# A planner's estimate of VectorE's times, made again, in a two-layer decoder step on one core

## The chip, the core and the metric

The kernel runs on one core of a Trainium2 chip. The metric is the device time of one execution in microseconds (us). The kernel before takes 2676.59 us, the median of three runs (2676.18 to 2676.59). Five engines work side by side, each through its own queue in program order: TensorE (PE in the profile) multiplies matrices, VectorE (DVE) and ScalarE (ACT) compute element by element, GpSimd (POOL) does a few small copies, and SyncE (SP) issues nearly all transfers from and to HBM.

## The reference, cut to what matters

It is one inference step of a two-layer trunk for 256 prompt tokens and 8 x 8 sample tokens, 320 in all, which share all weights, in fp32:

```
layer 0: x += chunk_mlp(rmsnorm(x))      # z = gelu(h @ w_in); u, v = z; v = rmsnorm(v)
                                         # s = causal mix of v per 128-token chunk; (u * s) @ w_out
         x += conv_ffn(rmsnorm(x))       # a = h @ w_in (2 x 5632); causal conv over 3 tokens
                                         # (silu(gate) * up) @ w_out
layer 1: x += dsa(rmsnorm(x))            # q, k, v, iq, ik, iw = h @ w_in; q, k normalised; rope
                                         # score = sum_heads relu(iq . ik) * iw; top-k of 64 keys a query
                                         # softmax attention over the selected keys; @ w_o
         x += conv_ffn(rmsnorm(x))
```

The prompt's queries choose 64 of up to 256 keys, the sample's 66 of 264 (256 of them in a paged cache). The updated caches and states are outputs too. D_MODEL is 2048; there are 16 query heads and 4 key heads of 128, and 16 index heads of 64.

## The kernel before

Everything is held transposed, 128 features on the partitions and the 320 tokens along the free axis; a 2048-wide activation is 16 such tiles. The weights come from HBM in units of 1 MB (`raw`, 3 buffers, on SP's queue). Each unit is used in two halves. `split(n)` (line 1182 on) makes of a half a high part `wh` (ScalarE) and a low part `wl` (VectorE), both 128x1024; the activations are split likewise (`hh`, `hl` for normed inputs, `rh`, `rl` for the ring of inner activations), and each weight tile is multiplied in three passes: wh.hh, wh.hl, wl.hh. A half is eight such triples, 24 matmuls of 320 columns. `split(n + 2)` is issued at the start of half n.

The weight matmuls are a list of groups of (mostly) 512 output columns: first the gMLP (v, u, down-projections in three parts), then ConvFFN 0, then the attention layer (index queries, index key, k, v, four q groups, four output groups per key head), then ConvFFN 1. A group's output columns rotate through six PSUM banks `mm`; a new column needs the bank of the sixth column before it, so `S.ensure(("ev", nbank - 6))`. Two more banks, `sd`, serve the small matmuls.

All the rest is side work, written as generators: norm tiles, the norm's end (`norm_fin`: sum over features by a matmul with ones, then 3 Newton iterations for the reciprocal root), the gating, the convolution (`ff_tile`), the index scores and their top-k search (`index_prompt`, `index_sample`, `topk`), rope, attention, key and value loads. They enter the queues by `Side.pump()`, called after every second triple: it advances a clock by SLOT = 0.82 us and lets each task that is ready take one step. A task's first step after it is added as urgent (the reading of a PSUM column) always runs. Other steps wait while `full()`, that is while the planned load of DVE or ACT is over BACKLOG = 3.0 us ahead of the clock; steps without small matmuls also wait until their inputs' planned end is near the clock (AHEAD), those with small matmuls until it is SLACK = 0.9 us behind it, and at most two of these run in a pump. Where the main loop needs something that is not made yet, `ensure` pumps on until it is: its instructions then stand ahead of the next matmul, which really waits for them.

The loads come from prices. Every engine object is wrapped (`Engine`, line 149 for all its instructions in the profile): before it issues an instruction it calls `side.op(key, price(name, n))`, with n the elements of the output per partition. In `op` the operation ends at max(engine free, the task's last end + LATENCY) + its price, and the engine's load is set to that end. The price of `dve.max` (8 largest values) goes by its output of 8 columns.

Two places to know for the prediction. In the last down-projection of the gMLP (and in the attention's last output groups) each half of 24 matmuls completes two columns of x; each is added to x (`resid`) and then normed (`norm_tile`: ScalarE's hh and square, then VectorE's hl and the sum of squares). The first ConvFFN groups need `("h", st, kt)` for kt 0 to 15 in order, a half using four of them, two column pairs after each other; its columns can be read only after `norm_fin` has set `("rs", st)`. In the attention layer, `index_done` waits for both searches and for the key ropes (`"k"`); it adds the attention tasks, which first issue the loads of cached keys and values on SP's queue. `k_done` stores new_kT, then `fold(1)` loads the rope tables (c_ropeT) again and multiplies them by the q gain (`"gq"`), after which the q columns can be roped and give their buffers (`tB`, four) back.

Of the kernel before, what the change touches and what calls it, by code (L numbers as in the profile page):

```python
# [33 lines left out]
AHEAD = 0.3  # L34
SLACK = 0.9
STEPS = 2
LATENCY = 0.1
PE = -1


# [5 lines left out]
class Side:  # L46
# [21 lines left out]
    def op(self, key, t):  # L68
# [8 lines left out]
        if key == "dma":  # L77
# [3 lines left out]
            return  # L81
        end = max(free, c.t + LATENCY if c else 0.0) + t
        self.load[key] = end
# [48 lines left out]
class Engine:  # L132
# [5 lines left out]
    def __getattr__(self, name):  # L138
        f = getattr(self.engine, name)
        if name == "value_load":  # L140
            return f

        def call(*a, **k):
            out = k["out"] if "out" in k else a[0]
            n = 1
            for d in out.shape[1:]:
                n *= d
            self.side.op(self.key, self.price(name, n))
            return f(*a, **k)  # L149

        return call
# [4 lines left out]


def dve_price(name, n):
    return (n * (0.6 if name in ("tensor_copy", "tensor_scalar", "memset") else 1.04) + 90) / 1e3


def act_price(name, n):
# [12 lines left out]
def trunk(ctx: ExitStack, tc: tile.TileContext, i, o):  # L175
# [3 lines left out]
    pool = Engine(nc.gpsimd, S, "pool", pool_price)  # L179
    sp = Engine(nc.sync, S, "dma", dma_price)  # L180
    dve = Engine(nc.vector, S, "dve", dve_price)
    act = Engine(nc.scalar, S, "act", act_price)

# [1140 lines left out]
```

## Time and profile before

| | before |
|---|---|
| median of 3 runs | 2676.59 us |
| profiled execution, its own time | 2677.56 us |
| its span | 2675.8 us |
| TensorE busy | 2652.6 us (99%) |
| VectorE busy | 1603.3 us (60%) |
| ScalarE busy | 1130.5 us (42%) |
| granted TensorE clock, mean | 0.997 |
| DMA | 405.70 MB, mean 152 GB/s |

The span is the time from the profile's first to its last instruction; the execution's own time is a little longer. Matmuls overlap in the array, so a busy TensorE is one that has work, not one at its peak. The side work and all weight splits share one source line (149), so instructions are told apart by the tiles that they write and read: `wl`, `wh` are the splits, `mm` the weight matmuls, `sd` the small ones, `xT` the residual, `hl` the norm's low half, and `arena` everything else of the side work.

### The profile page before, as it was taken

How to read it: one execution, taken by the hardware profiler on the slowest of the kernel's cores; microseconds unless marked ns; L12 is line 12 of the kernel's file. 1: busy time of each engine (PE TensorE's matmuls, PEld its weight loads, DVE VectorE, ACT ScalarE, POOL GpSimd, SP SyncE). 2: the span in 40 equal slices, each digit the busy share in tenths (PEclk: the TensorE clock that was granted, in tenths of full speed). 3: DMA queues.
4: the chain of work that ended last, by engine and by line, in shares of the span. 5: the costliest groups of instructions: out<-in, count | busy, mean ns of one | idle time of the engine just before them, and what ended most of it. 6: DMA issues, size and time to landing. Idle time of an engine off the chain costs nothing.

```text
span 2675.8 us, 44338 instructions
## 1 busy us (share of the span) xinstructions
PE 2652.6 (99%) x18174; PEld 2621.7 (98%) x18174; DVE 1603.3 (60%) x2803; ACT 1130.5 (42%) x1572; POOL 135.1 (5%) x370
## 2 busy tenths in 40 slices
PE   8999999999999999999999999999999999999999
PEld 8999999999999999999998989999999999999999
DVE  6465577646645564566668676776555645654663
ACT  5433344434433443344453554544344434433442
POOL 0000001001000010010000000000000000100100
PEclk9999999999999999999999999999999999999999
DMA  6444454444444444444543644444444444444444
GB/s 230 142 144 141 143 170 142 153 147 151 149 153 146 153 147 154 146 151 161 173 147 99 198 144 145 134 156 158 142 156 144 158 142 157 142 158 142 157 157 132
DMA packets 220284, 405.70 MB, mean 152 GB/s; under 512 B 9330, under 2 KB 33394, under 8 KB 219826
## 3 DMA queue, kind: packets, MB, share of 16 engines
q1 hardware_dynamic: 219794, 402.58, 46.2%
q8 instruction: 142, 2.33, 0.4%
q14 instruction: 60, 0.49, 0.1%
q10 hardware_dynamic: 288, 0.30, 0.0%
HBM read 396.69 MB, written 6.16 MB: 151 GB/s over the span
## 4 chain that ended last, share of the span: by engine, by line
PE 94%; DVE 3%; DMA 1%; ACT 1%; SPq 1%; issue 1%; ACTq 0%; DVEq 0%
PE mm L149 91%; PE sd L149 3%; DVE arena L149 2%; DVE wl L149 1%; SPq L149 1%; DMA arena<-a_v_norm 0%; ACT wh L149 0%; ACT arena L149 0%; DMA raw<-a_w_in 0%; DMA out_new_v_prompt<-arena 0%; DMA raw<-b_w_in 0%; DVE xT L149 0%; ACT rh L149 0%; DVE rl L149 0%; ACTq L149 0%
## 5 line engine op out<-in xcount | busy, mean ns | idle before, releaser
L149 DVE TENSOR_TENSOR wl<-raw,wh 128x1024 fp32r<-128x1024 f32 (+1 forms) x724 | 883.5, 1221 | 862.4 <-ACT wh L149 861.5
L149 ACT ACTIVATE wh<-raw 128x1024 fp32r<-128x1024 f32 (+1 forms) x724 | 764.6, 1057 | 1257.6 <-PE mm L149 1054.6
L149 PE MATMUL mm<-hh,wh 128*128 128x320 f32 x3856 | 1200.7, 311 | 10.5 <-DVE arena L149 9.9
L149 PE MATMUL mm<-hh,wl 128*128 128x320 f32 x3856 | 1192.2, 309 | 2.7 <-DVE wl L149 2.7
L149 PE MATMUL mm<-hl,wh 128*128 128x320 f32 x3856 | 1191.7, 309 | 0.0
L149 PEld LDWEIGHTS mm<-hh,wh 128*128 128x128 f32 x3856 | 726.0, 188 | 18.1 <-issue 15.6
L149 PEld LDWEIGHTS mm<-hh,wl 128*128 128x128 f32 x3856 | 725.8, 188 | 4.2 <-DVE wl L149 4.2
L149 PEld LDWEIGHTS mm<-hl,wh 128*128 128x128 f32 x3856 | 726.1, 188 | 0.7
L149 PE MATMUL mm<-rh,wh 128*128 128x320 f32 x1920 | 597.5, 311 | 0.0
L149 PE MATMUL mm<-rh,wl 128*128 128x320 f32 x1920 | 593.4, 309 | 0.0
L149 PE MATMUL mm<-rl,wh 128*128 128x320 f32 x1920 | 593.3, 309 | 0.0
L149 PEld LDWEIGHTS mm<-rh,wh 128*128 128x128 f32 x1920 | 360.7, 188 | 1.2 <-issue 1.0
L149 PEld LDWEIGHTS mm<-rl,wh 128*128 128x128 f32 x1920 | 360.7, 188 | 0.2
L149 PEld LDWEIGHTS mm<-rh,wl 128*128 128x128 f32 x1920 | 360.4, 188 | 0.0
L149 ACT ACTIVATE arena<-arena 128x336 f32<-128x336 f32 (+6 forms) x464 | 243.8, 540 | 148.3 <-DVE arena L149 144.7
L149 POOL COPY arena<-arena 128x16 f32<-128x16 f32 (+1 forms) x352 | 127.7, 401 | 1962.6 <-DVE arena L149 1544.6
L149 DVE SCALAR_TENSOR_TENSOR arena<-arena 128x336 f32<-128x336 f32 (+5 forms) x436 | 220.4, 510 | 9.2
L149 DVE TENSOR_TENSOR xT<-mm,xT 128x320 f32<-128x320 f32 x240 | 116.1, 487 | 81.4 <-PE mm L149 81.2
L149 DVE TENSOR_TENSOR arena<-arena 128x320 f32<-128x320 f32 (+6 forms) x413 | 146.4, 385 | 25.0 <-ACT arena L149 13.6
L149 DVE TENSOR_TENSOR arena<-mm,arena 128x64 f32<-128x64 f32 (+2 forms) x417 | 127.5, 343 | 47.6 <-PE mm L149 47.4
L149 PE MATMUL sd<-arena 128*128 128x128 f32 (+7 forms) x718 | 101.6, 318 | 6.6 <-DVE arena L149 3.3
L149 PEld LDWEIGHTS sd<-arena 128*128 128x128 f32 (+2 forms) x718 | 73.3, 157 | 22.0 <-issue 7.3
(36 smaller groups left out, 390.6 us busy)
## 6 DMA issues: line engine op xcount, KB each, us to landing
raw<-f_w_in SPq DMA_DIRECT2D x176, 1024.0 KB, 5.1
raw<-f_w_out SPq DMA_DIRECT2D x88, 1024.0 KB, 5.1
raw<-b_w_in SPq DMA_DIRECT2D x33, 1024.0 KB, 5.3
raw<-a_w_in SPq DMA_DIRECT2D x31, 1024.0 KB, 5.5
raw<-a_w_out SPq DMA_DIRECT2D x16, 1024.0 KB, 5.1
raw<-b_w_o SPq DMA_DIRECT2D x16, 1024.0 KB, 5.2
arena<-cache_kT SPq DMA_DIRECT2D x64, 64.0 KB, 2.0
arena<-cache_v SPq DMA_DIRECT2D x64, 64.0 KB, 2.0
```

Of the source, the lines that this page charges most:

```text
L149: return f(*a, **k)
```

## The change

Three prices of the planner are changed: LATENCY from 0.1 to 0.2; the fixed part of every DVE operation from 90 to 150 ns, and for `match_replace` (the search's second half) to 290 ns; and `max` is counted by the width of its input instead of its output of 8. No instruction is added or taken away; the order in which the side work stands in the queues is planned with the new figures.

```
-LATENCY = 0.1
+LATENCY = 0.2
...
-            out = k["out"] if "out" in k else a[0]
+            out = k["in_"] if name == "max" else k["out"] if "out" in k else a[0]
...
 def dve_price(name, n):
-    return (n * (0.6 if name in ("tensor_copy", "tensor_scalar", "memset") else 1.04) + 90) / 1e3
+    if name == "match_replace":
+        return (n * 1.04 + 290) / 1e3
+    return (n * (0.6 if name in ("tensor_copy", "tensor_scalar", "memset") else 1.04) + 150) / 1e3
```

## Rows read from the trace of the kernel before

**Rows 1.** The page's first part: engine, busy us (share of the span), instructions.

```profile
PE 2652.6 (99%) x18174; PEld 2621.7 (98%) x18174; DVE 1603.3 (60%) x2803; ACT 1130.5 (42%) x1572; POOL 135.1 (5%) x370
```

**Rows 2.** Stretches: length, busy PE, PEld, DVE, ACT, POOL, PE clock, DMA share, GB/s.

```profile
409.00:1315.00 906.00, 905.61 (x6175) 905.64 (x6176) 524.66 (x836) 374.51 (x467) 64.09 (x174) 1.00 0.46 151
...
1428.00:1476.00 48.00, 46.23 (x298) 41.60 (x296) 45.38 (x123) 16.75 (x28) 0.00 (x0) 1.00 0.34 110
1476.00:1506.00 30.00, 29.70 (x201) 29.34 (x200) 12.63 (x18) 12.29 (x20) 0.00 (x0) 1.00 0.76 245
...
1547.00:1562.00 15.00, 12.21 (x86) 9.35 (x85) 10.67 (x43) 9.82 (x28) 0.25 (x2) 0.92 0.48 145
1562.00:1592.00 30.00, 28.14 (x223) 25.04 (x222) 22.45 (x77) 16.76 (x38) 0.15 (x1) 0.98 0.42 126
```

**Rows 3.** Waits of PE: for whom, us in total, times, longest.

```profile
PE mm L149 <- DVE arena L149: 9.9, 3, 8.2
...
PE mm L149 <- DVE wl L149: 2.7, 5, 0.7
```

**Rows 4.** PE's time line, head and ConvFFN starts: start, us, instruction [idle before].

```profile
48.48 0.61 PE L149 MATMUL mm<-hh,wh 128*128 128x320 f32 x1 [8.20 <-DVE arena L149]
...
49.15 0.47 PE L149 MATMUL mm<-hh,wl 128*128 128x320 f32 x1
49.42 0.47 PE L149 MATMUL mm<-hh,wh 128*128 128x320 f32 x1
...
398.13 0.70 PE L149 MATMUL sd<-arena 128*128 128x320 f32 x2
...
409.39 0.39 PE L149 MATMUL mm<-hh,wh 128*128 128x320 f32 x1 [0.87 <-DVE arena L149]
...
1774.58 0.39 PE L149 MATMUL mm<-hh,wh 128*128 128x320 f32 x1 [0.87 <-DVE arena L149]
```

**Rows 5.** VectorE's time line at the first ConvFFN's start.

```profile
392.50 0.54 DVE L149 SCALAR_TENSOR_TENSOR hl<-xT,arena,hh 128x320 fp32r<-128x320 f32 x1
...
398.39 1.23 DVE L149 TENSOR_TENSOR wl<-raw,wh 128x1024 fp32r<-128x1024 f32 x1 [2.29 <-ACT wh L149]
...
400.78 0.49 DVE L149 TENSOR_TENSOR arena<-arena 128x320 f32<-128x320 f32 x1
401.30 1.02 DVE L149 SCALAR_TENSOR_TENSOR arena<-arena 128x320 f32<-128x320 f32 x2
...
408.69 1.94 DVE L149 TENSOR_TENSOR arena<-mm,arena 128x256 f32<-128x256 f32 x8
```

**Rows 6.** Groups by line and form, DVE: count, busy us, mean ns, idle before.

```profile
L149 DVE TENSOR_TENSOR wl<-raw,wh 128x1024 fp32r<-128x1024 f32 x720 | 880.8, 1224 | 861.2 <-ACT wh L149 860.3
```

**Rows 7.** VectorE's time line in the attention stage.

```profile
1434.02 0.42 DVE L149 MAX8 arena<-arena 128x8 f32<-128x256 f32 x1
...
1435.00 0.43 DVE L149 MAX8 arena<-arena 128x8 f32<-128x256 f32 x1
...
1497.37 0.89 DVE L149 TENSOR_SCALAR arena<-arena 128x320 f32<-128x320 f32 x2 [0.32 <-DMA arena<-c_ropeT]
...
1512.48 0.48 DVE L149 TENSOR_TENSOR arena<-mm,arena 128x320 f32<-128x320 f32 x1
```

**Rows 8.** The chain that ended last: start, us, engine and tile, instructions.

```profile
1774.58 897.84 PE mm L149 x6120
```

**Rows 9.** SP's queue in the attention stage: start, us, transfers issued.

```profile
1475.49 0.50 SPq L149 DMA_DIRECT2D out_new_kT<-arena  x1
...
1478.25 6.77 SPq L149 DMA_DIRECT2D arena<-cache_kT  x8
...
1494.99 0.91 SPq L149 DMA_DIRECT2D arena<-c_ropeT  x2
```

**Rows 10.** PE's time line in the attention stage.

```profile
1515.59 0.64 PE L149 MATMUL sd<-arena 128*32 128x256 f32 x8
...
1558.65 4.23 PE L149 MATMUL sd<-arena 128*128 128x128 f32 x14 [2.10 <-DVE arena L149]
```

## The prediction

> **What bounds the kernel now.** First the page's engine lines: TensorE is busy 2652.6 of a span of 2675.8 us [rows 1]. The matmuls of the weight groups fix the length; all else must fit beside them, and the 23 us in which TensorE stands still are what a better order can win. Second, the table by stretches of time, for where they lie: in the first ConvFFN (409 to 1315 us) TensorE misses 0.4 of 906 us; in 1428 to 1476, where VectorE (DVE) runs the top-k search, DVE is busy 45.4 of 48 us and TensorE misses 1.8; it misses 0.3 in 1476 to 1506, 2.8 in 1547 to 1562 and 1.9 in the 30 us behind that [rows 2]. Third, TensorE's waits: 9.9 us for DVE's arena work in three waits, of which one is 8.2 long, and 2.7 us for the low halves wl of the split weights [rows 3]. Fourth, TensorE's own time line: the 8.2 us are the first norm's tail at 48.48; the other two, 0.87 each, stand at 409.39 and 1774.58, the starts of the two ConvFFNs [rows 4].
>
> So three places can move: the two ConvFFN starts, which are alike, and the attention stage (1390 to 1592). Instructions, bytes and matmuls stay the same; the prices only set in which order the planner writes side work into the queues.
>
> **What the change does to the prices.** A DVE operation of 320 columns is priced 320 x 1.04 + 90 = 423 ns before and 483 after; one that hangs on the operation before it costs 0.523 and then 0.683 with LATENCY, which goes into DVE's load. In the norm's iterations the first such operation starts at 400.78 and its successor at 401.30: 0.52 us apart [rows 5]. The bare price becomes right, the chained one 30% too dear. A split of 1024 columns goes from 1.155 to 1.215; measured 1.224 [rows 6], right. A search round over 256 columns goes from 0.098 + 0.356 + 2 x 0.1 = 0.654 to 0.416 + 0.556 + 2 x 0.2 = 1.372; the trace has 1434.02 to 1435.00, 0.98 us [rows 7]: 33% too cheap before, 40% too dear after. All 25 rounds (8 of 256 columns, 9 of 264, 8 of 128): 15.3 before, 32.3 after. The 256 and 264 rounds at 0.98 and the 128 ones at some 0.7 (my estimate, scaled from these rows) make 22.
>
> An over-priced DVE does this: when its planned load is more than 3.0 us ahead of the clock, the planner holds every task that is not urgent. The side work then comes later against the matmuls, until a matmul needs it; there the planner pumps on without TensorE's progress, and TensorE really waits.
>
> [...]
>
> **Term 1, the ConvFFN starts.** In the eight halves of the last down-projection each half plans a split and two columns, each a residual add and a norm step (low half of h, sum of squares): 1.155 + 2 x (0.423 + 0.946) = 3.89 us before, 1.215 + 2 x (0.483 + 1.166) = 4.51 after, against 4 pumps x 0.82 = 3.28 us of clock. So the planned load overruns in both and the norm tiles are held. The extra: 16 x 0.28 for the columns, 0.54 for the four memsets of the ConvFFN's preparation, some 13 x 0.06 for splits, 5.8 us together. It drains at 3.28 - 1.215 = 2.07 a half, so the last tile comes 2.8 halves later: a half is 24 matmuls, 24 x 0.147 = 3.52 us [rows 8], so 10 us. Now the last low half is made at 392.50 [rows 5]. It is needed in the first group's seventh half, three halves ahead of the stall at 408.4 (409.39 less its gap), so at some 397.8. Slack 5, delay 10: the planner must make it there, behind that half's split, which ends at 399.6 [rows 5]. TensorE waits 1.2 to 2.4 us.
>
> Then the norm's reduction: 5.6 us from the last tile to its matmul (398.13, [rows 4]), and evictions at 408.69, 16 us from that tile [rows 5]. From about 400.3 this would end at 416, while the second group's second half, which needs a freed PSUM bank, comes at 408.4 + 2 = 410.4. What is left is then written in one go behind a split: two or three iterations of 1.56, a split 1.22, evictions 0.5 to 1, so 5.9 to 7.4 us of stall where there are 0.87 idle, 1.2 with the refill, now [rows 4]. Per start +1.2 to 2.4 and +4.7 to 6.2, so 5.9 to 8.6; I take 7, twice: **+14**. Bounds: the stalls of 1.2 vanish (-2.4), or the upper ends and a slow clock at both (2 x 8.6 + 2 x 2.9 = +23).
>
> On that clock: after the 8.2 us gap matmuls start 0.27 apart (49.15, 49.42) [rows 4] instead of 0.147 (897.84 / 6120, [rows 8]). 24 slow matmuls cost 24 x 0.12 = 2.9 us, and I keep that for the upper bound. [...]
>
> **Term 2, attention.** Search +17.0 and the 32 score accumulations +32 x 0.16 = 5.1: at least 22 us of planned DVE work more between 1390 and 1476, where the planner already holds. Of 0.82 us a pump the splits take 1.215 / 4 = 0.30; 22 / 0.52 = 42 pumps, or 37 us of TensorE's progress, by which the end of search and key work (new_kT is stored at 1475.49, [rows 9]) slides. Two matmul points wait for it. First, the third q group's second half needs a bank of the second q group, whose columns wait for the first group's rope buffers, and those for the query tables (c_ropeT). In the trace its first eviction is at 1512.48 [rows 7], and that half runs six matmuls behind the row at 1515.59 [rows 10], at about 1517: slack 4.5 us, far under 37. The wait holds what is left of the key ropes, 2 to 3 us; the tables, issue to use 2.4 us and more (1494.99 to 1497.37 [rows 7, 9]); one rope and an eviction, 2.5: some 7 to 8. The 24 cache loads that SP issues from 1478.25 to 1494.9, ahead of the tables [rows 9], add up to 17 if they fall into the wait again. Second, the first output group waits for attention 0 already now: its last 14 small matmuls take 1558.65 to 1562.9 and hold a wait of 2.10 for DVE [rows 10]. Starting later it is short by 5 to 8 more. The values' transposes, behind the search, may stall q0's banks for 0 to 5. Against it stand shorter waits for wl, 2 to 3 us of the 2.7 [rows 3] and of the 1.8 in 1428 to 1476 [rows 2]. Sum 7.5 + 6.5 + 2.5 - 2.5 = 14, and a quarter of the 17 for the loads: **+18**. Bounds: all of TensorE's idle time there gone (1.8 + 0.3 + 2.8 + 1.9 = -6.8), or everything at its upper end with the loads (+40).
>
> **Sum.** 14 + 18 = 32 on the profiled execution of 2677.6 is 2709.6; the median lies 1 us under it: 2709. The head (48.48) and the ConvFFNs' steady parts, where DVE has slack, cost nothing.
>
> **Rivals.** (1) Both places pay, my forecast: 2709, its own range 2695 to 2722; 0.45. (2) Only the ConvFFN starts pay, since search held back fills DVE's idle time in 1476 to 1506 (busy 12.6 of 30, [rows 2]) and the tables go ahead of the cache loads: 2677 + 14 = 2691; 0.18. (3) The cache loads fall in the wait whole: 2709 + 13 to 20, about 2726; 0.12. (4) The order hardly changes because urgent tasks and forced ones carry it, so the change doesn't do what it says: 2677, within 5; 0.10. For it speaks that most of the run is steady; against it that the plan is over its bound at all three places. (5) The other side: truer split and eviction prices bring wl in time and the idle 6.8 us in attention go with the 2.4 of the starts, 2677 - 9 = 2668; 0.15. It decides on the slack of 5 us at the ConvFFN starts: if the delay is under 1.4 halves instead of 2.8, no start pays, and term 2 must be nil too.
>
> 0.2% (5.4 us) is about what can be told from no change. Slower: 0.45 + 0.18 + 0.12 = 0.75; same 0.10; faster 0.15. The range 2671 to 2736 leaves out the better part of (5) and the worst of (3), about 0.2.
>
> **What would show it.** Right: TensorE waits for DVE at both ConvFFN starts, a short one for hl in the first group and one of 5 us or more in the second; a new wait in the third q group; DVE less dense in 1434 to 1476 and its search running past 1490; the wait for attention 0 longer. Wrong: the last hl still at least 3 us ahead of its use, search ending by 1480, or new idle time somewhere else, say in the gMLP's gating (before 376 us), for which I plan none.

## The result and the profile after

The changed kernel takes 2734.39 us, the median of four runs (2732.93 to 2736.72), against 2676.39 for the kernel before (2676.0 to 2676.59): the ratio is 1.0217, 95% interval 1.0205 to 1.0229, so 58 us slower. The forecast was 2709, with a range of 2671 to 2736.

The page's first part, of the profiled execution after the change (it answers to [rows 1]):

```profile
span 2732.7 us, 44318 instructions
...
PE 2671.2 (98%) x18174; PEld 2634.5 (96%) x18174; DVE 1618.0 (59%) x2803; ACT 1126.2 (41%) x1572; POOL 77.8 (3%) x370
```

The span grew by 56.9 us; the matmuls are the same 18174. The stretches that answer to [rows 2], and three new ones (length, busy PE, PEld, DVE, ACT, POOL, clock, DMA share, GB/s):

```profile
1428.00:1476.00 48.00, 48.00 (x336) 43.68 (x335) 36.13 (x71) 18.48 (x27) 0.00 (x0) 1.00 0.34 110
1476.00:1506.00 30.00, 30.00 (x207) 27.85 (x207) 21.35 (x57) 13.60 (x28) 0.00 (x0) 1.00 0.44 134
1506.00:1533.00 27.00, 20.13 (x123) 17.45 (x121) 21.56 (x55) 8.51 (x12) 0.00 (x0) 0.90 0.65 208
1561.00:1598.00 37.00, 24.59 (x131) 15.90 (x130) 21.13 (x87) 20.83 (x58) 0.42 (x2) 0.63 0.26 78
...
1572.00:1583.00 11.00, 9.82 (x50) 6.33 (x50) 6.15 (x36) 5.71 (x17) 0.16 (x1) 0.50 0.07 19
```

DVE is no longer dense in 1428 to 1476 (36.1 us instead of 45.4), and TensorE misses nothing there, nor in 1476 to 1506. The loss comes behind that: 6.9 us missed in 1506 to 1533, and 12.4 in 1561 to 1598, at a mean granted clock of 0.63. TensorE stands still for 8.99 us up to 1572.28, and in 1572 to 1583 its clock is 0.50.

TensorE's waits (answers to [rows 3]; us in total, times, longest):

```profile
PE mm L149 <- DVE arena L149: 23.4, 4, 8.2
PE sd L149 <- DVE arena L149: 19.9, 6, 9.0
PE mm L149 <- DVE hl L149: 3.8, 4, 1.7
PE mm L149 <- DVE rl L149: 1.8, 2, 0.9
PE mm L149 <- DVE wl L149: 1.8, 4, 0.7
```

Waits for DVE's arena work more than tripled (43.3 us of mm and sd together; before, 9.9 of mm and 3.3 of sd), and waits for hl are new; the gain in the waits for wl is 0.9 us. TensorE's time line at both ConvFFN starts, at the third q group and at the first output group (answers to [rows 4, 10]; in brackets the idle time before the instruction):

```profile
392.65 0.41 PE L149 MATMUL mm<-hl,wh 128*128 128x320 f32 x1 [1.75 <-DVE hl L149]
...
406.91 0.70 PE L149 MATMUL sd<-arena 128*128 128x320 f32 x2
417.99 0.60 PE L149 MATMUL mm<-hh,wh 128*128 128x320 f32 x1 [5.97 <-DVE arena L149]
418.39 0.47 PE L149 MATMUL mm<-hl,wh 128*128 128x320 f32 x1
418.66 0.47 PE L149 MATMUL mm<-hh,wl 128*128 128x320 f32 x1
...
1248.38 0.42 PE L149 MATMUL mm<-rh,wh 128*128 128x320 f32 x1 [0.53 <-ACT rh L149]
1249.68 0.41 PE L149 MATMUL mm<-rl,wh 128*128 128x320 f32 x1 [0.88 <-DVE rl L149]
...
1527.79 2.47 PE L149 MATMUL sd<-arena 64*128 64x320 f32 x4 [4.12 <-DVE arena L149]
1533.46 0.61 PE L149 MATMUL mm<-hh,wh 128*128 128x320 f32 x1 [3.20 <-DVE arena L149]
...
1572.28 2.66 PE L149 MATMUL sd<-arena 128*128 128x128 f32 x12 [8.99 <-DVE arena L149]
...
1597.08 0.41 PE L149 MATMUL mm<-rh,wh 128*128 128x320 f32 x1 [0.53 <-ACT rh L149]
...
1710.71 0.61 PE L149 MATMUL sd<-arena 128*128 128x128 f32 x3 [4.23 <-DVE arena L149]
...
1802.71 0.41 PE L149 MATMUL mm<-hl,wh 128*128 128x320 f32 x1 [1.70 <-DVE hl L149]
...
1828.02 0.60 PE L149 MATMUL mm<-hh,wh 128*128 128x320 f32 x1 [5.97 <-DVE arena L149]
```

The two ConvFFN starts are alike to 0.05 us: a wait for hl and one of 5.97 for the norm's end, where there were 0.87. After the latter, matmuls start 0.27 apart (418.39, 418.66), as after the long wait in the head. The pair at 1248 to 1250 is new as well: the last down-projection of ConvFFN 0 begins before its last inner tiles are made; ConvFFN 1 has the same.

VectorE's and SP's time lines that go with it (answers to [rows 5, 7, 9]):

```profile
392.05 0.55 DVE L149 SCALAR_TENSOR_TENSOR hl<-xT,arena,hh 128x320 fp32r<-128x320 f32 x1
...
400.04 0.55 DVE L149 SCALAR_TENSOR_TENSOR hl<-xT,arena,hh 128x320 fp32r<-128x320 f32 x1
...
414.14 0.48 DVE L149 TENSOR_TENSOR arena<-arena 128x320 f32<-128x320 f32 x1
...
415.71 0.49 DVE L149 TENSOR_TENSOR arena<-arena 128x320 f32<-128x320 f32 x1
...
417.29 1.94 DVE L149 TENSOR_TENSOR arena<-mm,arena 128x256 f32<-128x256 f32 x8
...
1525.79 0.42 DVE L149 MAX8 arena<-arena 64x8 f32<-64x264 f32 x1
...
1556.73 0.17 DVE L149 TENSOR_TENSOR arena<-arena 128x10 f32<-128x10 f32 x1
1556.93 0.38 DVE L149 SCALAR_TENSOR_TENSOR arena<-arena 128x10 f32<-128x10 f32 x2
```

```profile
1511.07 0.51 SPq L149 DMA_DIRECT2D out_new_kT<-arena  x1
1518.87 0.39 SPq L149 DMA_DIRECT2D raw<-b_w_in  x1
1519.30 0.98 SPq L149 DMA_DIRECT2D arena<-c_ropeT  x2
...
1526.53 4.84 SPq L149 DMA_DIRECT2D arena<-cache_kT  x8
```

The sixteenth low half comes at 400.04 instead of 392.50, the first evictions at 417.29 instead of 408.69, the sample's search ends at 1526 and new_kT is stored 36 us later.

To add this up, take the start of the n-th weight matmul (counted from 0) in each run's trace and subtract that of the kernel before. Four stages: up to the 2304th (the gMLP), the 8640th (ConvFFN 0), the 10992nd (attention) and the last one (ConvFFN 1). Differences in us:

| run | gMLP | ConvFFN 0 | attention | ConvFFN 1 | all | median, ratio (95%) |
|---|---|---|---|---|---|---|
| changed kernel | -0.5 | +12.6 | +32.3 | +12.4 | +56.8 | 2734.39, 1.0217 (1.0205 to 1.0229) |
| LATENCY alone (e1) | +0.4 | +8.1 | +4.9 | +6.4 | +19.9 | 2697.61, 1.0078 (1.0061 to 1.0094) |
| fixed part alone (e2) | -0.2 | +7.6 | +3.2 | +7.4 | +17.9 | 2694.85, 1.0070 (1.0053 to 1.0087) |
| search alone (e3) | -1.1 | 0.0 | +28.5 | 0.0 | +27.4 | 2704.61, 1.0104 (1.0087 to 1.0121) |
| LATENCY and fixed part (e4) | -0.5 | +13.5 | +25.5 | +12.2 | +50.7 | 2730.81, 1.0204 (1.0187 to 1.0221) |
| search, tables first (e5) | 0.0 | 0.0 | +18.4 | 0.0 | +18.3 | 2696.08, 1.0077 (1.0060 to 1.0094) |
| changed, bound 6.0 (e6) | -0.7 | +6.9 | +22.5 | +7.5 | +36.2 | 2714.31, 1.0143 (1.0126 to 1.0160) |
| measured prices (e7) | +0.2 | +7.4 | +20.9 | +7.0 | +35.5 | 2708.70, 1.0116 (1.0099 to 1.0133) |
| measured prices, clock 0.88 (e8) | -1.2 | -1.1 | +10.7 | -1.1 | +7.3 | 2688.49, 1.0047 (1.0030 to 1.0063) |
| the same, bound 6.0 (e9) | +2.7 | -1.1 | +9.6 | -1.1 | +10.0 | 2687.57, 1.0041 (1.0028 to 1.0055) |
| before, tables first (e10) | -0.4 | 0.0 | -6.7 | 0.0 | -7.1 | 2670.25, 0.9976 (0.9966 to 0.9986) |
| before, clock 0.92 (e11) | -2.3 | -1.1 | -0.2 | -1.1 | -4.8 | 2673.23, 0.9990 (0.9981 to 0.9999) |
| before, clock 0.88, bound 4.0, tables first (e12) | -0.8 | -1.1 | +2.3 | -1.1 | -0.7 | 2676.98, 1.0000 (0.9991 to 1.0009) |

Stages are those of one profiled execution, which need not be the median one: that of e4 lies 2.5 us under its median, that of e7 4.4 over it and that of e8 3.6 under it. The last column is of all runs, against those of the kernel before on the same chip (2675.86, 2676.42 and 2676.65 in three sets).

### The profile page after: what moved, and what is told of

Same layout as the page of the kernel before. It is cut to its first block, busy times and chain, and to the rows that moved or that the text cites. A ratio compares the mean times of both kernels' runs of the same rounds, so it can differ in the third digit from the quotient of the medians.

```text
span 2732.7 us, 44318 instructions
## 1 busy us (share of the span) xinstructions
PE 2671.2 (98%) x18174; PEld 2634.5 (96%) x18174; DVE 1618.0 (59%) x2803; ACT 1126.2 (41%) x1572; POOL 77.8 (3%) x370
## 3 DMA queue, kind: packets, MB, share of 16 engines
q1 hardware_dynamic: 219794, 402.58, 45.4%
## 5 line engine op out<-in xcount | busy, mean ns | idle before, releaser
L149 ACT ACTIVATE arena<-arena 128x336 f32<-128x336 f32 (+7 forms) x464 | 239.4, 539 | 127.8 <-DVE arena L149 125.5
L149 PE MATMUL sd<-arena 128*128 128x128 f32 (+8 forms) x718 | 108.8, 341 | 24.3 <-DVE arena L149 19.9
L149 POOL COPY arena<-arena 128x18 f32<-128x18 f32 (+1 forms) x352 | 69.9, 237 | 2019.2 <-DVE arena L149 1589.8
```

## The experiments

**The three prices one by one.** The theory: the planner's load for chained VectorE work is too high, so that it holds side work back until a matmul must wait. The rival: the search's price carries attention's loss alone, and the small fixed terms do little.

```
e1:  -LATENCY = 0.1                       e2:  -... else 1.04) + 90) / 1e3
     +LATENCY = 0.2                            +... else 1.04) + 150) / 1e3
```

> The kernel before with LATENCY 0.2 alone. Theory (planned load of chained VectorE work holds the side work back): a norm step costs 0.1 more in the plan, 16 x 0.1 + 0.3 for the memsets = 1.9 us at 2.13 a half, 0.9 halves later, so each ConvFFN start loses 1 to 3 us, attention 8 to 15 in the wait for attention 0; about 2692. Rival (the search's new price carries the loss in attention, the small fixed terms little): under 2682.

> The kernel before with the fixed part 150 alone. Theory: 16 x 0.12 + 0.24 + 13 x 0.06 = 2.9 us planned more, 1.4 halves, so each ConvFFN start loses 1 to 3 us; attention 8 to 15; about 2690. Rival (search's price): under 2682.

Both lie some 5 us above the theory's total (+21.7 and +19.0 by the medians), and its parts are off by more. The ConvFFN starts lose more than the 1 to 3 us expected. In the run with LATENCY alone:

```profile
393.58 0.41 PE L149 MATMUL mm<-hl,wh 128*128 128x320 f32 x1 [1.30 <-DVE hl L149]
414.92 0.39 PE L149 MATMUL mm<-hh,wh 128*128 128x320 f32 x1 [4.39 <-DVE arena L149]
```

With the fixed part alone there is no wait for hl, and the same 4.39 for the norm's end. Attention loses only 3 to 5, less than the 8 to 15 expected. By its number (under 2682) the rival falls with both, but through the ConvFFN starts; what it says of attention is not touched before e4.

```
e3:  +            out = k["in_"] if name == "max" else k["out"] if "out" in k else a[0]
     ...
     +    if name == "match_replace":
     +        return (n * 1.04 + 290) / 1e3
```

> The kernel before with the two search prices alone (max by its input, match_replace + 290). Theory: both ConvFFN starts stay as before (0.87 us of idle each), the search slides by some 33 pumps, a new wait in the third q group and a longer one for attention 0, together 10 to 20; about 2690. Rival (the search carries nearly all of attention's loss): 30 us or more in attention, 2706 or more.

The starts stay to the tenth, as expected; attention loses 28.5, between the theory's 10 to 20 and the rival's 30. One wait makes half of it, and SP's time line shows what it hangs on:

```profile
1527.94 0.60 PE L149 MATMUL mm<-hh,wh 128*128 128x320 f32 x1 [14.41 <-ACT arena L149]
```

```profile
1502.19 0.50 SPq L149 DMA_DIRECT2D out_new_kT<-arena  x1
1502.89 6.89 SPq L149 DMA_DIRECT2D arena<-cache_kT  x8
1509.96 4.64 SPq L149 DMA_DIRECT2D arena<-cache_v  x8
1514.78 3.93 SPq L149 DMA_DIRECT2D arena<-cache_kT  x8
...
1519.26 0.97 SPq L149 DMA_DIRECT2D arena<-c_ropeT  x2
```

The tables wait for 24 cache loads, my third rival. In the changed kernel they go ahead of the loads (1519.30 against 1526.53), so there this isn't the cause.

```
e4: the changed kernel with
-            out = k["in_"] if name == "max" else k["out"] if "out" in k else a[0]
+            out = k["out"] if "out" in k else a[0]
-    if name == "match_replace":
-        return (n * 1.04 + 290) / 1e3
```

> The changed kernel with the search's old prices (LATENCY 0.2 and the fixed part 150 stay). Theory: the ConvFFN starts lose all that they lose with the whole change, 12 us each, and attention most of its loss, since attention 0 itself is made of chained small operations: 2720 to 2733. Rival (search carries attention's loss): only the two starts, about 2701.

As the theory said: 2730.81, of the 58 us all but some 3; with that the rival falls for attention too. The search's price, which costs 28.5 by itself, adds little on top of the other two: 3 us by the medians, 6.8 in attention by the traces (32.3 - 25.5, with e4's trace 2.5 under its median). The losses in attention don't add. As I read it, without a run that shows it, each slides the end of the key work and of the search against matmul points that are the same. In the ConvFFN starts, LATENCY and fixed part come near their sum (8.1 + 7.6 = 15.7 against 13.5; 6.4 + 7.4 = 13.8 against 12.2).

**Is it SP's queue, in the run with the search's price?** The edit lets `k_done` issue the tables' loads before "k" is set, and so before the attention tasks can issue theirs.

```
e5: as e3, and
         sp.dma_start(o["new_kT"], kT)
+        f = fold(1)
+        d = next(f)
         S.set("k")
-        yield 1
-        yield from fold(1)
+        yield d
+        yield from f
```

> The kernel before with the search prices alone (that was 28.8 us slower, with one wait of 14.4 us in the third q group), and in it the rope tables' loads issued ahead of the 24 cache loads. Theory (the tables stand behind 16.4 us of cache loads on SP): that wait falls under 3 us, and since attention 0 starts as much sooner, the gain stays: about 2692. Rival (the wait is for the key ropes on VectorE, or is handed back in the wait for attention 0): 2700 or more.

```profile
1503.78 1.39 SPq L149 DMA_DIRECT2D arena<-c_ropeT  x2
1505.42 6.63 SPq L149 DMA_DIRECT2D arena<-cache_kT  x8
```

```profile
1519.91 0.61 PE L149 MATMUL mm<-hh,wh 128*128 128x320 f32 x1 [5.34 <-ACT arena L149]
```

The tables come 15.5 us sooner, the wait falls from 14.41 to 5.34, not under 3, and the stage by 10 us, which stay to the end (9.1 us by the medians: 28.8 against 19.7). 2696.08 lies between the theory's 2692 and the rival's 2700. 18 us stay that the queue doesn't explain, 15 of them between the 9870th and the 10032nd matmul, in the wait for attention 0.

**Is it the bound on the planned load?**

```
e6: the changed kernel with
-BACKLOG = 3.0
+BACKLOG = 6.0
```

> The changed kernel with the bound on the planned load at 6.0 instead of 3.0 us. Theory (this bound is what holds the side work): no wait for hl at the ConvFFN starts, the wait for the norm's end 3 us instead of 6.3, attention better by 5 to 10 us: about 2712. Rival (tasks come late since their planned inputs come late, whatever the bound): 2728 or more.

Measured 2714.31; the waits for hl are gone, that for the norm's end is smaller, and the third q group waits longer:

```profile
412.19 0.61 PE L149 MATMUL mm<-hh,wh 128*128 128x320 f32 x1 [4.39 <-DVE arena L149]
...
1531.50 0.60 PE L149 MATMUL mm<-hh,wh 128*128 128x320 f32 x1 [10.79 <-DVE arena L149]
```

Nothing but the bound differs, so the bound holds the tasks; 20 us of 58 come back. The longer wait in the third q group isn't the bound's alone: in this run new_kT is stored at 1507.82, the cache loads follow from 1508.57 on, and the tables come behind them, at 1524.30, as in e3. A second way in which the price can work is not tested by any run: a task is also not ready before the planned end of its inputs. One wait speaks for it, that for ConvFFN 0's last inner tiles (1248 to 1250): it costs 1.9 with the bound at 6.0 as it costs 2.0 at 3.0, and nothing with the measured prices of e7.

**Does a true price give a good order?**

```
e7: the changed kernel with                     e8: as e7, and
-LATENCY = 0.2                                  -SLOT = 0.82
+LATENCY = 0.04                                 +SLOT = 0.88
-        return (n * 1.04 + 290) / 1e3
+        return (n * 1.04 + 200) / 1e3
```

> The changed kernel with LATENCY 0.04 and match_replace at 200 instead of 290, so that a chained operation costs 0.523 (0.52 measured) and a search round of 256 columns 0.962 (0.98 measured). Theory (overpricing makes half of the loss; the rest comes of the clock of 0.82 us a pump, under TensorE's real 6 x 0.147 = 0.88): no wait for hl, 4 us at each ConvFFN start, 15 to 20 in attention, about 2702. Rival (the prices alone matter, and true ones give the best order): 2677 or less.

> As the one before, and the clock at 0.88 us a pump, TensorE's measured pace. Theory: the ConvFFN starts as in the kernel before or better; attention 8 to 15 slower, since a plan that is held to 3 us of load gives VectorE no more work ahead than that: about 2687. Rival (a true estimate is enough): 2677 or less.

With prices as measured the kernel still loses 32 us; setting the planner's clock to the measured pace as well gives 20 of them back and makes the ConvFFN starts 1.1 us better than in the kernel before. Both came out near what the theory had, 2708.70 (about 2702 expected; the starts cost 7 each instead of 4) and 2688.49 (2687). So the low prices of the kernel before made up for a clock of 0.82 that runs behind TensorE's 0.88: a half's plan was 3.89 against 3.28 of clock there, a ratio of 1.19; with measured prices it is 1.215 + 2 x (0.483 + 1.006) = 4.19, 1.28; in the changed kernel 4.51, 1.38; with the clock at 0.88 it is 4.19 against 3.52, 1.19 again. The ratio is not the whole of it: by the same sums e1 has 1.25 and e2 1.31, and ConvFFN 0 loses 8.1 and 7.6 there against e7's 7.4. In e7's attention the tables fell behind the cache loads once more:

```profile
1523.99 0.91 SPq L149 DMA_DIRECT2D arena<-c_ropeT  x2
```

```profile
1529.76 0.61 PE L149 MATMUL mm<-hh,wh 128*128 128x320 f32 x1 [9.05 <-ACT arena L149]
```

```
e9: as e8, and  -BACKLOG = 3.0
                +BACKLOG = 6.0
```

> The changed kernel with measured prices (LATENCY 0.04, match_replace 200), the clock at 0.88 us a pump and the bound at 6.0. Theory (with true prices and pace only the bound of 3 us kept VectorE short of work in attention): the third q group no longer waits, the wait for attention 0 is half of what it was with the bound of 3, the starts stay: about 2678. Rival (true prices cost attention for another reason): 2686 or more.

2687.57: the theory's 2678 is missed, and the rival stands. With true prices and pace some 10 us of attention's loss are not due to the bound. The third q group no longer waits, as expected (3.7 us in e8), but TensorE now waits 4.5 us in five places from 1408 to 1478, among the index scores and the search (0.2 in e8), and the gMLP is longer too (+2.7 us instead of -1.2). What the 10 us are due to stays open. One candidate stands in both traces and wasn't tried on them: the tables come behind the 24 cache loads again (in e9 at 1506.56, with the first cache load at 1489.99). In e8 new_kT is stored at 1487.27, the first cache load follows at 1487.79, and then:

```profile
1504.87 0.97 SPq L149 DMA_DIRECT2D arena<-c_ropeT  x2
```

**A better order than both.** e10 is the kernel before with e5's edit alone, e11 the kernel before with `SLOT = 0.92`, e12 with `SLOT = 0.88`, `BACKLOG = 4.0` and e5's edit.

> The kernel before with the rope tables' loads issued ahead of the 24 cache loads. Theory (the tables stood 17 us behind cache loads, and attention 0, which waited for the ropes, is what the first output group waits for): most of the 8 us at the first output group go: about 2670. Rival (attention 0 is bound by its own work, or the cache loads come late in turn): 2675 or more.

> The kernel before with the clock at 0.92 us a pump: less is held, the opposite direction of the change. Theory: the stalls of 1.2 us at both ConvFFN starts go, the wait for attention 0 shrinks by 3 to 6, against more waits for wl in the search of 2 or 3: about 2671. Rival (the order before is at its best, more work ahead costs as much as less): 2678 or more.

> The kernel before with the clock at 0.88, the bound at 4.0 and the tables first. Theory: the gains of the two before it add up in part: about 2667. Rival: 2675 or more.

The tables first make the kernel before faster by 0.24% (2670.25; interval 0.14 to 0.34%). They are issued at 1475.59, and the first output group starts 5.7 us sooner in its trace (1556.81 instead of 1562.54, the start of the 10032nd weight matmul):

```profile
1475.59 1.42 SPq L149 DMA_DIRECT2D arena<-c_ropeT  x2
...
1479.26 6.27 SPq L149 DMA_DIRECT2D arena<-cache_kT  x8
```

```profile
1547.00:1562.00 15.00, 14.66 (x106) 13.76 (x105) 10.86 (x41) 10.48 (x25) 0.00 (x0) 1.00 0.47 142
```

The 2.8 us that TensorE missed in that stretch are 0.3. The planner's faster clock in e11 gains 0.10%, in the gMLP (2.3 us) and at the ConvFFN starts; in attention, 2.8 us less of waiting before the first output group stand against 5.5 more within the search. e12 missed: at 2676.98 the gains don't add. With more search ahead of it on DVE, TensorE waits inside the search, here in e12:

```profile
1453.71 0.41 PE L149 MATMUL mm<-hh,wl 128*128 128x320 f32 x1 [1.16 <-DVE wl L149]
...
1462.88 1.44 PE L149 MATMUL sd<-arena 128*128 128x320 f32 x2 [3.96 <-DVE arena L149]
```

So work ahead can be overdone in attention just as it can be held too long.

## Why the prediction was right, and where its sizes were off

The direction, the three places and the way they lose were right: a too dear chained operation, side work held, matmuls that wait for it. The amount was not: 32 us were summed and 57 measured, outside the 2695 to 2722 of the likeliest case, though inside the whole range by 1.6 us. That it lies inside is luck: the upper end made room for rival (3), which is not what happened in the changed kernel. Term by term:

- **Prices.** "The bare price becomes right, the chained one 30% too dear" held for 320 columns (at 414.14 an operation takes 0.48 us, and the next, which hangs on it, starts 0.52 behind it): with LATENCY cut to 0.04, 25.7 us of the medians' difference of 58.0 went (together with the search's 0.09 a round). But the smallest operations were left out of the working. The rows of 10 columns above start 0.20 apart; a chained one is priced 10 x 1.04 + 150 + 200 = 360 ns, 80% too dear, and attention has 48 operations of 10 columns and some 50 of one or two.
- **Term 1**, sized at 7 a start, measured 12.6 and 12.4. The wait for hl was placed in the first group's seventh half; it came in the fifth (TensorE stops at 390.9, 4.3 halves of 3.52 behind the group's start at 375.6), for tile 10 and the one behind it, and cost about 4 with the slow matmuls after it (0.27 apart from 394.31 on; the 2448th matmul 4.0 later against the 2304th) instead of 1.2 to 2.4. I had taken the last tile as the one that is late, and the delay as one that grows up to it. But the hold delayed tile 10 most: its low half is ready 13.6 us later (at 392.60 instead of 379.01), more than the 12.2 us that it came ahead of its use before. The last one is only 7.5 us later (400.04 instead of 392.50), with 6.2 ahead of its use, and by then TensorE itself was 4 behind. The norm's end cost 6.7 more (2496th to 2544th), just over the 4.7 to 6.2: 5.1 of idle time and 1.5 of the slow clock, which stood in the upper bound only, there with 24 slow matmuls (12 are slow here, 0.27 apart instead of 0.147). That range was also summed wrongly: two or three iterations of 1.56, a split of 1.22 and 0.5 to 1 make 4.8 to 6.9 us of stall, not 5.9 to 7.4, and so 3.6 to 5.7 more than before; the 5.1 of idle time lie inside that. The 1.56 was an estimate, three times the 0.52 of [rows 5]; an iteration measured 1.57 (414.14 to 415.71). What stands in the 5.97 is a split and two iterations (414.14 and 415.71 in the rows above). Evictions came at 417.29, where 416 was worked out. And 2.0 stood in no term: the wait for ConvFFN's last inner tiles (1248 to 1250), in a part said to cost nothing because DVE has slack. DVE has it (busy 528.7 of 910 us from 418 to 1328), the plan has not.
- **Term 2**, sized at 18, measured 32.3 (-6.8 to +40 as its bounds). The slide was right: new_kT comes 36 us later, where 37 was worked out. The new wait in the third q group is there and has its size: 7.3 us of idle time between the 9678th and the 9864th matmul (4.12 and 3.20 in the rows above), 0.3 before, where 7.5 stood. What stands in it is the sample search's end, not the tables or the cache loads. (That stretch is 14 us longer, but 6 of them are small matmuls that stood earlier before; from the 8640th to the 9678th the changed kernel is 9.8 us ahead.) The mis-sized step is the first output group: "short by 5 to 8 more" was 18 (9870th to 10032nd: 16.6 to 34.5 later). I had let attention 0 start a little later; it was made almost whole inside the wait, 35.5 us without a weight matmul (1561.57 to 1597.08) at a clock of 0.63. Of the 18, 9.6 are idle time and 8.4 are small matmuls that take longer, though there are no more of them (136 instead of 139). Behind it 14 come back (10038th to 10224th), but only because 123 small matmuls fewer stand there: they come later, and 23 are lost in the fourth q group and the two output groups after it, for which I had no term. The shorter waits within the search were there (TensorE misses nothing in 1428 to 1506 after, 2.1 before).
- **Term 2, the clock.** The slow clock stood in no part of this term. Over the whole stage the 32.3 are 20.3 of idle time and 12.2 by which the same 670 small matmuls take longer (from a start to the next, less idle time): 104 of them run at the lower clock (0.50), 9 before, and there one of 128 columns takes 0.21 us instead of 0.11.
- **Rivals.** (2) falls, as attention pays the larger part. (3) is not what happened in the changed kernel, but the tables did come behind the loads in e3, e6, e7, e8, e9 and e11, as in the kernel before. It hangs on which ends last: in all of these new_kT is stored after the sample search's last round (in e3 at 1502.19, with that round at 1471.59); in the changed kernel, e1, e2 and e4 the search ends later than that (1511.07 and 1525.79), and the tables go first. (4) falls. (5) falls here: the slack of 5 us at the ConvFFN starts was not enough; e8, whose ratio of plan to clock is that of the kernel before, has starts that are better by 1.1, as (5) would have it.

What is shown: that the starts' loss is made by LATENCY and the fixed part and not by the search (e1 to e4), that the bound and the clock make a part of it (e6, e8), and SP's queue in e3. What is only argued: how attention's 32 us divide between the three prices, since they don't add. What costs e8 and e9 their last 10 us is open, since the tables were not put first in them.

## What to carry to other kernels

A planner's prices are worth something only together with its clock and its bounds: one of them made truer can make the order worse, so compare the planned work of a stage with the planned time of the same stage before and after, and look for the first consumer whose slack is smaller than the slide. A task that is held doesn't save its engine's time (VectorE was busy 1618.0 us after, 1603.3 before); it moves the work into a place where TensorE waits for it, and here the small matmuls behind a wait of 8.99 us ran at a clock of 0.50 as well. And before prices are tuned, look for an order that is left to chance: two loads put ahead of 24 others gained more here than any price, clock or bound that was tried.

## What the runs showed that was not expected

Losses in attention don't add up: 4.9, 3.2 and 28.5 us one by one, 25.5 for the first two together and 32.3 for all. And two waits of the same kind came out as equal numbers in different kernels, 4.39 us in e1, e2 and e6 and 5.97 in the changed kernel, in e4 and in e7: what is left of the norm's end when the wait begins is a split and a whole number of its iterations, one in e1 (at 412.65 in its trace), two in the changed kernel (414.14 and 415.71). So a stall of this kind moved in steps of 1.58 us (5.97 - 4.39), about one iteration (1.57 between these two), and not evenly with the price.
